# A kernel whose instruction order is planned at build time, planned with other durations

## Chip, cores and metric

One core of one Trainium2 chip runs the whole kernel in one launch. The metric is the device time of an execution in microseconds (us); less is better. The kernel before was timed three times.

## What is computed

A batch of one, 256 tokens by 1024 channels, in float32, goes through two blocks. The first has four layers, each a residual around a mixer: a convolution mixer (layer A), forgetting attention (B), a short convolution (C), and the convolution mixer again (A). The second has two layers, each a token mixer of two attentions and then a feed-forward part with a short convolution.

```
for i in range(4):                      # first block
    kind 0: x = x + conformer_conv_mixer(rms_norm(x, a_norm[j]), ...)       # 31 taps, 2048 channels
    kind 1: x = x + forgetting_attention_mixer(rms_norm(x, b_norm[j]), ...) # 16 heads of 128
    kind 2: x = x + short_conv_mixer(rms_norm(x, c_norm[j]), ...)           # 3 taps
for l in range(2):                      # second block
    x = layer_norm(ALPHA * x + g1 * token_mixer(x * (1 + sc1) + sh1), ...)
    x = layer_norm(ALPHA * x + g2 * conv_ffn(x * (1 + sc2) + sh2), ...)     # 2 x 2816 channels, 3 taps
```

## The kernel before

**Recording and planning.** The Python program does not issue instructions as it goes. Every operation is recorded as an `Op` (`Graph.add`, line 162) with the engine or engines that may run it, a duration that `cost` (line 514) or `mm` (line 624) gives it, the operations it needs, and a key. The key is `Graph.clock`, the sum of the durations of the products recorded so far, plus a shift in microseconds. `Graph.schedule` (line 208) then plays the whole program through: whenever an engine is free, `pick` (line 285) gives it the ready operation with the lowest key whose buffers can be had. An operation is ready when what it needs has ended in the plan and a latency has passed: `SELF`, `CROSS` and `TO_PE` (lines 125 to 127) hold these by engine; for a DMA it is 1.9 us to ACT, DVE or Pool and 2.1 us to TensorE. `issue` (line 457) writes the instructions out in the planned order of start. On the chip each engine runs its own list in that order and waits on semaphores. So a duration in the plan never reaches the chip as a time: it decides the order on each engine, the engine of the few operations that have a choice, the buffer slots, and how many idle products are put in.

**What the plan leaves open.** When TensorE has nothing ready, `schedule` may add an idle product (`idle_op`, line 432), a small product of zeros that nobody reads. An operation with two engines goes to the second if the first would be later (`pick`).

**The work.** Weights come by DMA from SP in tiles of 128x1024 float32 (`need`, line 647), into five slots `wr`. A weight tile is then split into a high and a low part: ACT copies it to `wh` (rounded), and the difference goes to `wl`. The difference is DVE's work, or that of DVE or Pool in layers A and C (`FLEX`, line 577). A product of 128x128 by 128x256 is made of three: high by high, high by low, low by high (`mm3`, line 635). In layer A, 13 of 24 pairs of chunks skip the split and use plain float32 products (`NATIVE_A`, line 550), so that each of the two layers A has 38 tiles whose difference may be on either engine. The DMA of a tile has a key three `LEAD` (4.45 us, line 552) ahead of its product, and the split one.

**Layer A's convolution** (`conv`, line 1023). The last taps of a channel chunk are products on ACT (tile `tap`) that Pool adds up (tile `C`); DVE then adds the first taps on top, in PSUM (tile `po`) and back into `C`. The first of these DVE instructions reads two SBUF tiles, the others one. All these have keys `CONV` (33.45 us, line 553) late. TensorE then sums `C` over the channels (`sums`).

**Layer C** also works out a position bias for later (`bias_block`, line 995): DVE writes masks (`msk`, SBUF to SBUF), TensorE multiplies them with a table.

**Modulation** (`modulate_all`, line 930): 192 DMAs of 128x512 (tile `wa`, two slots) each feed one DVE instruction, beside layer B and the first token mixer.

```
    def need(src, kind="split"):
        with G.late(-3 * LEAD):
            w = G.tile("weights", [128, 1024], F32, "wr", "wr")
            sp.dma_start(w, src)
...
        with G.late(-LEAD):
            a.activation(h, w, AF.Copy)
            (dp if flex[0] else v).tensor_tensor(l, w, h.bitcast(F32), op=OP.subtract)
        return [h, l]
```

Of the kernel before, what the change touches and what calls it, by code (L numbers as in the profile page):

```python
# [9 lines left out]
F32R = mybir.dt.float32r  # L10
# [11 lines left out]
class Buf:  # L22
    """A tile before it has a place: what its instructions are is known, not yet when they run."""
# [8 lines left out]
class View:  # L32
    """A part of a tile: the same steps lead to it in numpy's indices and, later, in the tile's."""
# [58 lines left out]
    def region(self):  # L92
        """First and last partition, and first and last element in them."""
        a = self.arr
        off = a.__array_interface__["data"][0] - self.buf.start
        row = self.buf.row
        p, f = divmod(off, row)
        ext = sum((n - 1) * s for n, s in zip(a.shape[1:], a.strides[1:]))
        return p, p + a.shape[0], f, f + ext + 1
# [16 lines left out]
class Op:  # L116
    __slots__ = ("i", "choices", "key", "need", "outs", "bufs", "fresh", "table", "group", "start", "end", "eng", "waits", "args", "kw",
                 "fn", "done", "margin", "base", "hurry", "act")


class Graph:
    """Instructions with what they need of each other, put in an order that keeps the engines busy."""

    # from the end of an instruction to the start of one that needs it
    SELF = {"PE": 0.0, "DVE": 0.127, "ACT": 0.153, "Pool": 0.102, "DMA": 0.0}
    CROSS = {"PE": 0.2, "DVE": 0.15, "ACT": 0.15, "Pool": 0.12, "DMA": 1.9}
    TO_PE = {"DVE": 0.3, "ACT": 0.36, "Pool": 0.25, "DMA": 2.1}
    # TensorE's clock doubles after a window with so much work for the array, and halves after one with so little
# [33 lines left out]
    def add(self, choices, fn, outs, ins, args, kw, key=None, group=None):  # L162
# [8 lines left out]
        o.table = TABLE.get(args[2]) if fn == "activation" else None  # L171
        o.bufs = []
        pe = choices[0][0] == "PE"

        def meets(e, r, psum):
            # a bank counts as one, save for TensorE alone
            return psum and not (pe and e[4]) or e[0] < r[1] and r[0] < e[1] and e[2] < r[3] and r[2] < e[3]
# [30 lines left out]
    def schedule(self):  # L208
# [14 lines left out]
        # an accumulating product may begin with any of its parts: each may claim the bank  # L223
# [30 lines left out]
        def turn(t):  # L254
            """Goes on to the window of time t."""
            nonlocal tick, load, warm, after
            n = int(t / self.TICK)
            while tick < n:
                warm = load >= self.DOWN if warm else load >= self.UP
                tick, load, after = tick + 1, after, 0.0  # L260

        def room(o):
            """Whether the tiles that begin with this instruction can have their slots."""
            for b in o.bufs:
                if b.slot is not None or b.tag not in free:
                    continue
                n = len(free[b.tag])
                q = queue[b.tag]
                while q and q[0][2].slot is not None:
                    heapq.heappop(q)  # L270
                if n == 0 or (n <= self.reserve.get(b.tag, 1) and q[0][2] is not b):
                    return b.tag
            return None
# [3 lines left out]
        def blocked(o, e, t):  # L277
            """Whether something more urgent comes up before this would be through."""
            end = t + dict(o.choices)[e]
            for w, k, i in soon[e]:  # L280
                if t < w < end - self.HOLD[1] and w < t + self.HOLD[0] and not ops[i].done and k < o.key[0] - self.HOLD[2] and room(ops[i]) is None:
                    return True
            return False
# [57 lines left out]
        latest, count = 0.0, len(ops)  # L341
        t = 0.0
# [3 lines left out]
        while left or events:  # L346
            for e in ENG:
# [25 lines left out]
                if e == "PE":  # L373
                    turn(t)
                    work = o.act
                    if not warm:
                        d = max(0.107, 2 * d)
                        work *= 2
                    over = min(work, max(0.0, t + work - (tick + 1) * self.TICK))
                    load += work - over  # L380
                    after += over
                o.start, o.end = t, t + d
# [49 lines left out]
    def idle_op(self, tag):  # L432
        """A product of zeros that nothing reads: it keeps TensorE's clock up while there is nothing to do."""
# [6 lines left out]
        o.need, o.group, o.outs, o.done, o.table, o.margin, o.hurry = set(), None, [ps], False, None, 0.0, 0.0  # L440
# [49 lines left out]
class Engine:  # L490
    """Records an engine's instructions; their first argument, or out, is what they write."""
# [21 lines left out]

def cost(eng, fn, out, ins, args, kw):
    """The time of an instruction, about, in microseconds."""
    if eng == "DMA":
        some = out if isinstance(out, View) else ins[0]
        return max(0.45, some.shape[0] * some.numel() * 4 / 350e3)
# [61 lines left out]
def program(G, A, V):  # L580
# [43 lines left out]
    def mm(out, w, m, group=None):  # L624
        n = m.numel()
        if m.dtype == F32:
            us = max(0.214, 0.005 + n / 600.0)
        else:
            us = max(0.107 if n < 128 or m.dtype == BF else 0.056, 0.0025 + n / 2400.0)
# [41 lines left out]
    def dense(ps, half, src, kind="split", m=None):  # L671
        """One chunk of 128 outputs, channels by tokens, into half a bank."""
# [15 lines left out]
    def tokens512(srcs, m=None):  # L688
        """512 outputs, tokens by channels: a bank for each half of the tokens."""
# [15 lines left out]
    class Out:  # L705
        """1024 outputs of a product over n chunks, in four banks; the last chunks bank by bank."""
# [27 lines left out]
        def finish_chunks(self, on_chunk):  # L734
            """Chunk by chunk; what is left of the last one goes to a bank of its own, to be added to the rest."""
# [83 lines left out]
    def sums(st, i, src, grp, n):  # L819
        """Adds a chunk's sums over channels, over n, to the columns 2i, 2i+1 of st, a row for each token."""  # L820
# [4 lines left out]
    def rows(cols, n):  # L825
        """[128 tokens, n] columns, as a row for each pair of them, the same on every partition."""
# [6 lines left out]
    class Sums:  # L833
        """Means over channels, of chunks of which all but the last two are added up first."""
# [23 lines left out]
    def raw_tiles(kind):  # L858
        """Places for the next layer's input before its division by the norm, which its first products take."""
# [29 lines left out]
    def mean_rstd(st, eps):  # L889
        """From columns of means and of means of squares, the mean and 1/std of each token as rows."""  # L890
# [8 lines left out]
    def residual(out, gain=None, i0=0, late=0.0, raw="split"):  # L899
        """Adds a mixer's output to x, and takes the next layer's norm."""  # L900
# [29 lines left out]
    def modulate_all(l, after, step, late):  # L930
        """A modulation's columns, a sum over a row of weights each."""
# [20 lines left out]
    def positions():  # L952
# [9 lines left out]
        # the steps of the bias from bucket to bucket, 8 times as large, in three bfloat16 parts  # L962
# [32 lines left out]
    def bias_block(t, i0, n):  # L995
        """The bias (8 times as large) of the queries of half t and the keys 4 i0 .. 4 (i0 + n)."""
# [13 lines left out]
    def layer_a(j, raw):  # L1010
# [12 lines left out]
        def conv(c):  # L1023
            """The last taps by products on ACT and sums on Pool, then the rest on top by DVE, in PSUM."""
# [85 lines left out]
    def softmax(lt, t, p, scale, bias_of=None):  # L1110
        """Exponentials of a head's logits for 128 queries, over their sum."""
# [19 lines left out]
    def head(logits, vt, scale, p, alloc, bias_of=None):  # L1131
        """One head: logits(out, t, n) writes those of 128 queries."""
# [16 lines left out]
    def layer_b(raw):  # L1149
# [14 lines left out]
        def forget():  # L1164
# [18 lines left out]
            # rows of -c and c for every head, in three bfloat16 parts on partitions 0, 32 and 64  # L1183
# [143 lines left out]
    def residual_norm(out, l, gi, gain, shift, nxt):  # L1327
        """x = norm(x + g y), and the next product's input from it; x is kept ALPHA times as large."""
# [39 lines left out]
    def mixer(l):  # L1368
# [20 lines left out]
        # indexer queries, and the chunk of indexer keys and rope keys  # L1389
# [19 lines left out]
        # latent queries and keys  # L1409
# [24 lines left out]
        # queries of the selected attention  # L1434
# [4 lines left out]
        # scores of the keys, and the 64 best of them  # L1439
# [67 lines left out]
        # keys and values of the selected attention, and the gates, beside the attention itself  # L1507
# [170 lines left out]
def layouts(i):  # L1678
    """The inputs as the kernel reads them: transposed, permuted and repeated, never changed."""
# [132 lines left out]
```

## Time and profile before

| | us |
|---|---|
| three timed runs | 1862.46, 1865.36, 1860.3 |
| their median | 1862.46 |
| the profiled execution, span from its first to its last instruction | 1860.9 |

The page gives no other time for the profiled execution than its span; what lies around the span is not shown, and 1860.9 lies among the three runs. Every recorded instruction is issued from one helper, so that all have line L487, and tiles tell them apart: `pd`, `pa` and `po` are PSUM banks, `wr`, `wh`, `wl` a weight tile and its parts, `hh`, `hl`, `ph`, `pl` the parts of the other factor, `C`, `tap`, `U` the convolution's, `idle` the idle products. In time the stages are layer A from 0 to about 200 us, B to 545, C to 815, A to 1000, then mixer, feed-forward, mixer (from 1465), feed-forward (from 1660).

### The profile page before, as it was taken

The page shows a single profiled execution, that of the slowest core. Times are in us where ns is not written, and L with a number is a line of the kernel's source. Part 1 is how long each engine was busy: PE and PEld are TensorE (multiplying, and loading weights), DVE is VectorE, ACT ScalarE, POOL GpSimd, SP SyncE. Part 2 cuts the span into 40 slices and gives each one's busy share as a digit, 9 for nine tenths or more (in the row PEclk, how much of TensorE's full clock was granted, in tenths as well). Part 3 has the DMA queues.
Part 4 walks back from the last instruction along what each step waited for, and adds up shares of the span by engine and source line. Part 5 has one row for each costly group of instructions (what it writes and reads, how often), then busy time and mean ns, then how long its engine had stood idle before and what let it go on. Part 6 is the DMA issues. An engine that isn't in the chain of part 4 may idle for free.

```text
span 1860.9 us, 37322 instructions
## 1 busy us (share of the span) xinstructions
PE 1792.5 (96%) x14150; PEld 1718.2 (92%) x14150; DVE 1498.7 (81%) x3251; ACT 1117.2 (60%) x1985; POOL 418.8 (23%) x487
## 2 busy tenths in 40 slices
PE   9989999999999999999889999999999999999998
PEld 8878999988898989999889988999999989999998
DVE  7998989877768766679999788799887885687766
ACT  6876555544554433468766657946555568766554
POOL 4998401000011032039984100000000100000000
PEclk9999999999999999999999999999999999999999
DMA  7433557877734544543336657666876343446661
GB/s 246 136 114 136 190 188 235 254 250 257 237 117 150 181 159 159 190 150 104 123 125 202 205 176 228 218 228 207 260 253 200 137 139 123 137 136 214 189 191 54
DMA packets 107172, 334.91 MB, mean 180 GB/s; under 512 B 12784, under 2 KB 13168, under 8 KB 106992
## 3 DMA queue, kind: packets, MB, share of 16 engines
q1 hardware_dynamic: 106992, 332.52, 55.2%
q8 instruction: 111, 1.82, 0.4%
q14 instruction: 69, 0.57, 0.1%
HBM read 331.43 MB, written 1.05 MB: 179 GB/s over the span
## 4 chain that ended last, share of the span: by engine, by line
PE 54%; DVE 8%; POOL 3%; ACT 3%; DMA 3%; issue 2%; ACTq 0%; POOLq 0%; SPq 0%; DVEq 0%
PE pd L487 33%; PE po L487 17%; PE pa L487 4%; POOL C L487 3%; DMA wa<-in_w_ada 2%; DVE po L487 2%; DVE wl L487 2%; PE idle L487 1%; ACT wh L487 1%; DVE wa L487 1%; ACT tap L487 1%; DVE msk L487 1%; DVE x L487 1%; DVE IQ L487 0%; ACT L487 0%
## 5 line engine op out<-in xcount | busy, mean ns | idle before, releaser
L487 ACT ACTIVATE wh<-wr 128x1024 fp32r<-128x1024 f32 x478 | 502.7, 1057 | 435.8 <-PE pd L487 289.9
L487 PE MATMUL pd<-hh,wh 128*128 128x256 f32 x2456 | 694.9, 285 | 4.8 <-DVE up L487 1.5
L487 PE MATMUL pd<-hh,wl 128*128 128x256 f32 x2456 | 686.0, 283 | 13.2 <-DVE wl L487 13.2
L487 DVE TENSOR_TENSOR wl<-wr,wh 128x1024 fp32r<-128x1024 f32 x452 | 567.6, 1262 | 155.5 <-ACT wh L487 153.4
L487 PE MATMUL pd<-hl,wh 128*128 128x256 f32 x2456 | 686.0, 282 | 1.5 <-DVE hl L487 1.5
L487 PEld LDWEIGHTS pd<-hh,wl 128*128 128x128 f32 x2456 | 465.6, 191 | 14.3 <-DVE wl L487 13.6
L487 PEld LDWEIGHTS pd<-hh,wh 128*128 128x128 f32 x2456 | 466.3, 190 | 10.1 <-ACT up L487 2.5
L487 PEld LDWEIGHTS pd<-hl,wh 128*128 128x128 f32 x2456 | 464.7, 190 | 4.4 <-DVE hl L487 1.9
L487 POOL TENSOR_TENSOR C<-C,tap 128x233 f32<-128x233 f32 (+16 forms) x364 | 263.2, 748 | 57.8 <-ACT tap L487 48.3
L487 PE MATMUL po<-pl,wh 128*128 128x256 f32 x904 | 253.8, 284 | 2.5 <-DVE pl L487 2.5
L487 PE MATMUL po<-ph,wh 128*128 128x256 f32 x904 | 255.8, 284 | 0.3 <-DVE ph L487 0.3
L487 PE MATMUL po<-ph,wl 128*128 128x256 f32 x904 | 255.4, 283 | 0.0
L487 DVE SCALAR_TENSOR_TENSOR po<-U,vec,po 128x246 f32<-128x246 f32 (+20 forms) x532 | 214.9, 469 | 1.1
L487 ACT ACTIVATE tap<-U,vec 128x227 f32<-128x227 f32 (+17 forms) x364 | 159.7, 480 | 49.2 <-POOL C L487 29.8
L487 PE MATMUL pd<-hn,wr 128*128 128x256 f32 x768 | 179.2, 388 | 1.0 <-DVE U L487 1.0
L487 PEld LDWEIGHTS po<-pl,wh 128*128 128x128 f32 x904 | 170.6, 190 | 2.8 <-DVE pl L487 2.8
L487 PEld LDWEIGHTS po<-ph,wh 128*128 128x128 f32 x904 | 171.5, 190 | 0.8 <-PE idle L487 0.6
L487 PEld LDWEIGHTS po<-ph,wl 128*128 128x128 f32 x904 | 171.7, 190 | 0.0
L487 PEld LDWEIGHTS pd<-hn,wr 128*128 128x128 f32 x768 | 145.1, 193 | 19.7 <-DVE U L487 1.1
L487 POOL TENSOR_TENSOR r<-r,neghalf 128x4 f32<-128x4 f32 (+1 forms) x22 | 28.2, 1281 | 315.7 <-DVE r L487 217.7
L487 POOL TENSOR_TENSOR wl<-wr,wh 128x1024 fp32r<-128x1024 f32 x26 | 63.0, 2424 | 152.0 <-ACT wh L487 150.0
L487 DVE CUSTOM_DVE_ANT_0 wa<-wa,scr,mods 128x512 f32<-128x512 f32 x96 | 72.3, 753 | 27.4 <-DMA wa<-in_w_ada 26.2
(273 smaller groups left out, 2540.2 us busy)
## 6 DMA issues: line engine op xcount, KB each, us to landing
wr<-in_a_in SPq DMA_DIRECT2D x96, 512.0 KB, 3.6
wa<-in_w_ada SPq DMA_DIRECT2D x192, 256.0 KB, 3.7
wr<-in_w_up SPq DMA_DIRECT2D x88, 512.0 KB, 4.4
wr<-in_c_in SPq DMA_DIRECT2D x64, 512.0 KB, 3.6
wr<-in_m_in SPq DMA_DIRECT2D x64, 512.0 KB, 4.0
wr<-in_b_in SPq DMA_DIRECT2D x48, 512.0 KB, 4.4
wr<-in_w_dn SPq DMA_DIRECT2D x44, 512.0 KB, 4.4
wr<-in_a_out SPq DMA_DIRECT2D x32, 512.0 KB, 4.2
```

The lines of the kernel that those rows point to most:

```text
L487: getattr(eng[o.eng], o.fn)(*args, **kw)
```

## The change

The durations that the planner uses are replaced, and a resource is added. A DMA's data is taken to be there 2.75 us (2.85 for TensorE) after its transfer instead of 1.9 (2.1), and a transfer runs at 340 GB/s instead of 350, with a least time of 0.2 us instead of 0.45. A split product over 256 columns takes 0.450 ns a column if its moving tile is a constant buffer and 0.462 ns otherwise (over 512 columns as well), instead of 0.0025 us and 2400 columns a us. A bfloat16 product of 128 columns or more has a lower least time. And Pool's `tensor_tensor` and those DVE instructions that read two SBUF tensors, or copy or scale from SBUF to SBUF, share a port in the plan: an instruction that is given to its engine while the other holds the port is made longer by the rest of the other's time. `pick` does not look at the port. Comments and docstrings are dropped. The rest of the program, its constants among it, is the same.

```diff
-    CROSS = {"PE": 0.2, "DVE": 0.15, "ACT": 0.15, "Pool": 0.12, "DMA": 1.9}
-    TO_PE = {"DVE": 0.3, "ACT": 0.36, "Pool": 0.25, "DMA": 2.1}
+    CROSS = {"PE": 0.2, "DVE": 0.15, "ACT": 0.15, "Pool": 0.12, "DMA": 2.75}
+    TO_PE = {"DVE": 0.3, "ACT": 0.36, "Pool": 0.25, "DMA": 2.85}
...
         o.table = TABLE.get(args[2]) if fn == "activation" else None
+        o.port = shared_port(choices[0][0], fn, outs, ins)
...
+        port = 0.0
         t = 0.0
         self.order = []
...
+                if e == "Pool" or e == "DVE" and o.port:
+                    if o.port and port > t:
+                        d += port - t
+                    if o.port:
+                        port = t + d
                 o.start, o.end = t, t + d
...
+def shared_port(eng, fn, outs, ins):
+
+    if eng == "Pool" or not outs:
+        return fn == "tensor_tensor"
+    sb = [x.numel() > 1 and x.buf.pool != "psum" for x in ins]
+    return eng == "DVE" and (sum(sb) > 1 or fn in ("tensor_scalar", "tensor_copy") and all(sb) and outs[0].buf.pool != "psum")
...
-        return max(0.45, some.shape[0] * some.numel() * 4 / 350e3)
+        return max(0.2, some.shape[0] * some.numel() * 4 / 340e3)
...
-            us = max(0.107 if n < 128 or m.dtype == BF else 0.056, 0.0025 + n / 2400.0)
+            us = max(0.107 if n < 128 else 0.039 if m.dtype == BF else 0.056, 0.0025 + n / 2400.0)
+            if m.dtype == F32R and n >= 256:
+                us = n * (0.450e-3 if m.buf.pool == "const" else 0.462e-3)
```

## Rows read from the trace of the kernel before

**Rows 1.** The page's first part: the span, and each engine's busy time.
```profile
span 1860.9 us, 37322 instructions
PE 1792.5 (96%) x14150; PEld 1718.2 (92%) x14150; DVE 1498.7 (81%) x3251; ACT 1117.2 (60%) x1985; POOL 418.8 (23%) x487
```

**Rows 2.** The chain that ended last, in feed-forward one: start, us, what.
```profile
1298.55 5.47 PE pd L487 x48
1304.03 2.81 PE po L487 x24
```

**Rows 3.** TensorE's waits, whole kernel: us in total, times, longest.
```profile
PE pd L487 <- DVE wl L487: 13.2, 3, 6.1
PE pa L487 <- DVE hd L487: 7.4, 8, 1.7
PE pa L487 <- DVE C L487: 7.3, 7, 2.9
PE pa L487 <- DVE msk L487: 6.1, 4, 1.5
PE pa L487 <- POOL r L487: 4.2, 6, 1.5
PE pa L487 <- DVE p L487: 2.9, 5, 1.1
PE po L487 <- DVE pl L487: 2.5, 1, 2.5
```

**Rows 4.** Timeline, first layer A: start, us, engine, what; DVE, then Pool, then TensorE.
```profile
135.28 6.88 DVE L487 TENSOR_TENSOR wl<-wr,wh 128x1024 fp32r<-128x1024 f32 x1
...
135.56 2.34 POOL L487 TENSOR_TENSOR wl<-wr,wh 128x1024 fp32r<-128x1024 f32 x1
137.87 3.21 POOL L487 TENSOR_TENSOR C<-C,tap 128x230 f32<-128x230 f32 x5
...
142.21 0.80 PE L487 MATMUL pd<-hh,wl 128*128 128x256 f32 x2 [6.10 <-DVE wl L487]
```

**Rows 5.** The same, second layer A: DVE, then TensorE.
```profile
932.20 8.71 DVE L487 TENSOR_TENSOR wl<-wr,wh 128x1024 fp32r<-128x1024 f32 x1
...
940.96 1.01 PE L487 MATMUL pd<-hh,wl 128*128 128x256 f32 x3 [5.91 <-DVE wl L487]
```

**Rows 6.** All of tile wr's and of tile msk's DVE instructions: ns minimum/median/maximum.
```profile
L487 DVE TENSOR_TENSOR wl<-wr,wh x452: 1207/1224/8710, 20.1 to 1830.6; 128x1024 fp32r<-128x1024 f32 x151
...
L487 DVE TENSOR_SCALAR msk<-posf,post x96: 268/280/2364, 325.4 to 748.9; 128x128 bf16<-128x128 f32 x96
```

**Rows 7.** Windows by time: us, busy (count) of PE, PEld, DVE, ACT, POOL; clock.
```profile
139.00:146.00 7.00, 3.79 (x17) 3.79 (x18) 7.00 (x12) 1.61 (x3) 3.05 (x6) 0.52 0.38 131
```

**Rows 8.** Timeline: masks in layer C, `pl` in the second layer A.
```profile
659.68 2.82 DVE L487 TENSOR_SCALAR msk<-posf,post 128x128 bf16<-128x128 f32 x3 [0.34 <-PE pa L487]
...
659.99 2.42 POOL L487 TENSOR_TENSOR wl<-wr,wh 128x1024 fp32r<-128x1024 f32 x1 [0.23 <-DVE msk L487]
...
992.64 2.57 DVE L487 TENSOR_TENSOR pl<-n,ph 128x256 fp32r<-128x256 f32 x1
...
992.53 2.40 POOL L487 TENSOR_TENSOR wl<-wr,wh 128x1024 fp32r<-128x1024 f32 x1 [0.89 <-PE pd L487]
```

**Rows 9.** Pool's groups: first layer A (0 to 200), second (815 to 1000).
```profile
L487 POOL TENSOR_TENSOR wl<-wr,wh 128x1024 fp32r<-128x1024 f32 x7 | 16.6, 2368 | 1.1 <-ACT wh L487 1.1
...
L487 POOL TENSOR_TENSOR wl<-wr,wh 128x1024 fp32r<-128x1024 f32 x6 | 14.9, 2491 | 1.4 <-PE pd L487 0.9 <-ACT wh L487 0.6
```

**Rows 10.** DMA issues (count, KB each, median us from issue to landing).
```profile
wr<-in_a_in SPq DMA_DIRECT2D x96, 512.0 KB, 3.6
...
wr<-in_w_up SPq DMA_DIRECT2D x88, 512.0 KB, 4.4
```

**Rows 11.** Tile wa: DVE's waits for it (us, times), and its DMAs' landing.
```profile
  DMA wa<-in_w_ada: 53.5, 63
...
DMA to landing us min/median/max: 2.3/3.7/7.4
```

More of the change, by code (lines that the diff above doesn't have):

```diff
@@ L117 @@
     __slots__ = ("i", "choices", "key", "need", "outs", "bufs", "fresh", "table", "group", "start", "end", "eng", "waits", "args", "kw",
-                 "fn", "done", "margin", "base", "hurry", "act")
+                 "fn", "done", "margin", "base", "hurry", "act", "port")
 class Graph:
     SELF = {"PE": 0.0, "DVE": 0.127, "ACT": 0.153, "Pool": 0.102, "DMA": 0.0}
-    CROSS = {"PE": 0.2, "DVE": 0.15, "ACT": 0.15, "Pool": 0.12, "DMA": 1.9}
-    TO_PE = {"DVE": 0.3, "ACT": 0.36, "Pool": 0.25, "DMA": 2.1}
+    CROSS = {"PE": 0.2, "DVE": 0.15, "ACT": 0.15, "Pool": 0.12, "DMA": 2.75}
+    TO_PE = {"DVE": 0.3, "ACT": 0.36, "Pool": 0.25, "DMA": 2.85}
     TICK, UP, DOWN = 4.096 / 1.2, 2.56, 1.28
@@ L439, in idle_op @@
         o.base = o.key = (0.0, o.i)
-        o.need, o.group, o.outs, o.done, o.table, o.margin, o.hurry = set(), None, [ps], False, None, 0.0, 0.0
+        o.need, o.group, o.outs, o.done, o.table, o.margin, o.hurry, o.port = set(), None, [ps], False, None, 0.0, 0.0, None
         o.bufs, o.fresh = [ps.buf, w.buf], []
```

## The prediction

> **What bounds the kernel now.** I read the page's busy shares first. TensorE is busy 96% of the span, DVE 81%, ACT 60%, Pool 23% [rows 1]: the kernel is made of products, and only what makes TensorE wait can be won by another order. Second, the chain that ended last shows what a product costs when nothing disturbs it. In the feed-forward parts it is nothing but products, 48 in 5.47 us and 24 in 2.81 us [rows 2], so 0.1140 and 0.1171 us each. There is nothing to win there. Third, TensorE's waits: the list is short, 43.6 us in its seven longest entries, and nearly all are waits for DVE [rows 3]. Fourth, the timeline around the largest two. In the first layer A a DVE subtraction `wl`, which has a median of 1.224 us [rows 6], lasted from 135.28 to 142.16, and TensorE stood still 6.10 us for it. All that time Pool added SBUF tiles without a pause: its own `wl`, then five taps, to 141.08; DVE ended 1.08 us later [rows 4]. The second layer A repeats it, 8.71 us and a wait of 5.91 us [rows 5]. Behind such a wait the granted clock falls: 0.52 of full from 139 to 146 [rows 7], nearly all of it at the level of 1.2 GHz; from 142.2 to 146 products ran at half pace, some 2 us lost, so 4 us for both. The same collision in small stands in layer C: a mask, 0.28 us at the median and 2.36 at worst [rows 6], is held behind a Pool `wl` (three masks in 2.82 us while Pool subtracted) [rows 8], four times in TensorE's list [rows 3].
>
> **The change, part by part.** No duration of the plan reaches the chip. The work stays the same but for idle products and for the engine of single `wl` and sums; what can change is order.
>
> *Longer products.* For 256 columns the plan took 0.0025 + 256/2400 = 0.1092 us; now 0.1152 (constant buffers) and 0.1183. The chip has 0.1140 and 0.1171 [rows 2], so the plan was 4 and 7% short and is now 1% long. On the chip this removes nothing. The keys grow with it, while `LEAD` stays 4.45 us: 38.6 products ahead instead of 40.8, a quarter of a microsecond less, for the split and threefold for the DMA. Only one of the three waits for `wl` is not a collision, at 13.2 - 6.10 - 5.91 = 1.2 us [rows 3, 4, 5]; this slack covers the loss. Where the order gets truer, the waits for `hd` and `r`, mostly in layer B, could shrink (7.4 + 4.2 = 11.6 us [rows 3]); a shuffled order could as well double them. Ends -11.6 and +11.6. I take 0, as these are chains between engines whose own durations are not changed.
>
> *Later landings.* A weight tile was planned at 524288 B / 350 GB/s + 1.9 = 3.40 us, now 1.54 + 2.75 = 4.29; the trace has 3.6 to 4.4 [rows 10]. For `wa` it was 2.65, now 3.52, beside a median of 3.7 [rows 11]. DVE stood 53.5 us, 63 times, in front of `wa` [rows 11], and what is queued behind it on DVE waits too. An honest landing puts other DVE work ahead. But TensorE felt little: its waits there are mainly those for `p`, 2.9 us [rows 3]. Ends 0 and -2.9; I take -1.5. SP's queue keeps its order within a pool of slots and is bound by free slots; I cost its reordering at nothing, since TensorE's seven longest waits name no DMA [rows 3]; without that cover one late tile costs the 0.9 us by which landings were misjudged.
>
> *Port, one Pool instruction ahead.* Where a DVE instruction meets a single Pool subtraction, the new charge is right: 2.82 us for three masks, and 2.57 for `pl` behind the `wl` that began 0.11 us before it [rows 8]. The plan now knows that these come late and gives TensorE other products first. That is the four waits for `msk`, 6.1 us, and the one for `pl`, 2.5 [rows 3]: -8.6, between 0 (the products offered instead are late as well) and -8.6. I take all, because in layer C TensorE has `po` products at hand.
>
> *Port, a train.* At 135.28 the charge would have been only the tap then running, 135.56 - 135.28 = 0.28 us, where DVE really lost 5.7 [rows 4]. The planner lets the two alternate; the chip let Pool go on. So the 6.10 + 5.91 + 4 = 16 us of the two large events are won only as far as the plan's ready times move. Ends 0 and -16. I take the part that one instruction explains, 2.34 of 6.88 us [rows 4], a third: -5.4. Likewise for the waits on `C`, 7.3 us [rows 3], a third, -2.5, ends 0 and -7.3.
>
> The Trainium skill, page "SBUF — State Buffer", section "SBUF: two separate sides", says that Pool and a DVE instruction with two SBUF inputs share a port pair as an exclusive lock, held for one whole instruction by whichever started first. The trace agrees that one blocks the other and not that it ends with one instruction: DVE waited through six [rows 4]. By that rule the train would be charged in full, and the sum would hold the third rival's figure.
>
> *Given back.* A new order of some thousands of instructions makes new waits. Nearest row: a collision in layer A, about 6 us [rows 4, 5]. I take one slightly smaller, +3.5, with ends 0 and +12 (two).
>
> **Sum:** -1.5 - 8.6 - 5.4 - 2.5 + 3.5 = -14.5 us. The profiled execution's span is 1860.9 us, which makes 1846.4; the median of the runs shown lies 1.6 above that span, so 1848.
>
> **Rivals.**
>
> *Only the places move.* The planner charges the port but does not avoid it, so that new collisions replace the old. For: `pick` is blind to the port, and Pool's `wl` come from the same rule. Against: the four masks are charged exactly. Time: 1862.
>
> *Slower: Pool gets more subtractions in layers A.* DVE's longer planned instructions make `pick` find DVE late more often, and the tile goes to Pool. There a `wl` takes 2.37 to 2.49 us against 1.22 [rows 6, 9], holds the port as long and leaves taps behind that run as a train. Layers A had 7 + 6 = 13 [rows 9] of 76 possible. These 13 cost TensorE 6.10 + 5.91 + 2.5 + 4 = 18.5 us [rows 3, 4, 5, 7], 1.4 each. With twenty more: +28 - 14.5 = +13.5, so 1876. It decides from ten more (14.5/1.4), and is visible from fourteen. Against: Pool also becomes busier in the plan, which keeps it from taking tiles.
>
> *All of the port is won.* If every collision is planned as it happens, the port terms go in full: 8.6 + 16 + 7.3 = 31.9, and with the landings 1.5, 1862.5 - 33.4 = 1829. It is what the rule of the Trainium skill's page "SBUF — State Buffer" would bring. Against it stand the six Pool instructions of [rows 4].
>
> That the change does not do what it says is a small case: an order that came out the same would give 1862, inside the first rival.
>
> **How the numbers follow.** Forecast 0.50, places only move 0.18, slower 0.20, all of the port 0.12. The forecast's own range, with the train between 0 and -16 and new waits between 0 and 12, is 1838 to 1857. The range over the cases reaches from below the third rival, 1824 (the `C` and `wa` waits in full and some of layer B's), to the slower one's 1876. A difference of 0.3%, 5.6 us, is about what a measurement of this kernel can tell from none; the three runs spread over 5. Faster: 0.12 + nearly all of 0.50, 0.60; same: 0.18 and a little, 0.19; slower 0.21.
>
> **What would show it.** Right: no TensorE wait for `msk` and `pl`; DVE's waits for `wa` under 20 us; the feed-forward chain still 5.47 and 2.81; Pool's `wl` in layers A near 13, with the longest DVE `wl` well under 8.7 us. Wrong: more than 23 `wl` of Pool there, or DVE instructions over 5 us beside Pool trains with TensorE waiting; or new waits of layer B's kind beyond 11.6 us, which would say that the truer product lengths cost slack that the old, short ones had left.

## The result, and the profile after

The kernel after takes 1831.83 us (median of 4 runs, 1829.68 to 1840.08) beside 1863.51 us for the kernel before (4 runs): the ratio is 0.9837, 95% interval 0.9812 to 0.9861, so 1.6% faster. The forecast was 1848: right in sign, with less than half of the gain. The time lies in the range over all cases, 1824 to 1876, but below the forecast's own range of 1838 to 1857, and, as the experiments show, it came largely for other reasons than mine.

The first part of the page of the kernel after:

```profile
span 1829.3 us, 38072 instructions
PE 1799.9 (98%) x14515; PEld 1725.9 (94%) x14515; DVE 1487.1 (81%) x3260; ACT 1117.5 (61%) x1986; POOL 417.6 (23%) x478
```

Beside [rows 1] the span is 31.6 us shorter. TensorE's 365 further instructions are idle products (851 instead of 486), and nine instructions went from Pool to DVE; the rest of the work is the same. The feed-forward chain (start, us, what) is what it was in [rows 2]:

```profile
1262.15 2.81 PE po L494 x24
1264.96 5.47 PE pd L494 x48
```

TensorE's waits in the kernel after (us in total, times, longest), to be read beside [rows 3]:

```profile
PE pa L494 <- DVE C L494: 3.4, 3, 2.1
PE idle L494 <- ACT Z L494: 2.4, 2, 2.2
PE pa L494 <- POOL r L494: 2.2, 2, 1.9
PE pa L494 <- DVE sel L494: 1.9, 2, 1.3
PE idle L494 <- DVE x L494: 1.8, 1, 1.8
PE pd L494 <- POOL wl L494: 1.4, 2, 1.1
PE pd L494 <- DMA wr<-in_a_in: 1.4, 1, 1.4
```

The seven longest add to 14.5 us instead of 43.6. The waits for `wl` on DVE, `hd`, `msk` and `pl` are gone. The instructions behind them, in the views of [rows 6] and [rows 11]: DVE's subtractions and masks (ns minimum/median/maximum), DVE's waits for `wa` (us, times).

```profile
L494 DVE TENSOR_TENSOR wl<-wr,wh x458: 1204/1225/3389, 20.7 to 1799.3; 128x1024 fp32r<-128x1024 f32 x153
...
L494 DVE TENSOR_SCALAR msk<-posf,post x96: 268/281/584, 302.6 to 726.9; 128x128 bf16<-128x128 f32 x96
...
  DMA wa<-in_w_ada: 27.2, 34
```

No subtraction is held for 7 or 9 us any more, no mask for 2.4, and the 53.5 us in front of `wa` are halved. The mean granted clock rose from 0.984 to 0.991 of full.

**Where the time went.** For the table I took in each trace the start of the last product that the program records for a layer; a stage is the time from one to the next. A is the whole convolution layer, the output part included; M and F are mixer and feed-forward part. All in us, from each run's profiled execution. By this measure the first layer A ends at 252 us in the kernel before and the second at 1042, later than in the rough stages given with its profile. The first stage begins 14.3 to 17.9 us after the start of the span, and the last ends 8 to 9 us before its end; these parts are not in the table.

| run | A1 | B | C | A2 | M1 | F1 | M2 | F2 |
|---|---|---|---|---|---|---|---|---|
| before | 237.9 | 310.4 | 248.0 | 231.5 | 216.3 | 192.2 | 207.5 | 194.6 |
| after | 235.2 | 300.0 | 239.3 | 224.2 | 211.8 | 192.7 | 211.1 | 191.9 |
| port_only | 236.4 | 308.8 | 249.1 | 227.9 | 211.3 | 193.1 | 206.6 | 191.0 |
| products_only | 236.6 | 321.2 | 239.3 | 229.1 | 222.7 | 195.0 | 212.0 | 191.6 |
| landings_only | 228.7 | 298.9 | 250.5 | 225.4 | 211.4 | 195.0 | 205.7 | 193.9 |
| without_port | 230.9 | 301.1 | 239.4 | 227.2 | 213.6 | 193.2 | 211.6 | 191.8 |
| without_products | 234.7 | 306.1 | 248.3 | 229.5 | 210.1 | 194.7 | 210.7 | 191.7 |
| without_landings | 234.9 | 324.7 | 239.8 | 240.0 | 215.9 | 192.1 | 211.6 | 192.1 |
| landing_wa | 235.6 | 293.0 | 250.4 | 232.8 | 210.4 | 194.5 | 208.9 | 192.5 |
| landing_weights | 233.7 | 308.6 | 249.6 | 227.8 | 213.8 | 191.7 | 207.7 | 193.1 |
| landings_no_pool_c | 229.7 | 298.3 | 240.8 | 225.4 | 209.7 | 193.3 | 209.4 | 191.6 |
| after_no_pool_wl | 227.6 | 303.5 | 237.5 | 217.8 | 210.7 | 194.5 | 210.4 | 191.5 |
| no_port_no_pool_wl | 228.8 | 301.7 | 239.0 | 226.4 | 212.7 | 193.2 | 210.2 | 192.1 |
| after_no_idle | 237.9 | 300.5 | 238.4 | 228.0 | 210.3 | 192.1 | 211.4 | 192.5 |

The change took 10.4 us from B, 8.7 from C, 7.3 from A2 and 4.5 from M1. From the first layer A, which had one of the two large collisions, it took 2.7; M2 became 3.6 us longer. The stages also show how much an order scatters where nothing is at stake: F1 and F2 lie between 191 and 195 in every run.

### The profile page after: what moved, and what is told of

Read it like the earlier page. It is cut to its first block, busy times and chain, and to the rows that moved or that the text cites. A ratio compares the mean times of both kernels' runs of the same rounds, so it can differ in the third digit from the quotient of the medians.

```text
span 1829.3 us, 38072 instructions
## 1 busy us (share of the span) xinstructions
PE 1799.9 (98%) x14515; PEld 1725.9 (94%) x14515; DVE 1487.1 (81%) x3260; ACT 1117.5 (61%) x1986; POOL 417.6 (23%) x478
## 4 chain that ended last, share of the span: by engine, by line
PE 79%; DVE 10%; ACT 4%; DMA 2%; POOL 2%; issue 2%; SPq 0%; POOLq 0%; DVEq 0%; ACTq 0%
PE pd L494 49%; PE po L494 22%; PE pa L494 7%; DVE po L494 4%; DVE wl L494 2%; PE idle L494 1%; POOL C L494 1%; ACT wh L494 1%; ACT L494 1%; DMA wa<-in_w_ada 1%; DVE IQ L494 1%; DMA wr<-in_a_in 1%; ACT tap L494 1%; DVE m L494 0%; DMA pi<-in_pos 0%
## 5 line engine op out<-in xcount | busy, mean ns | idle before, releaser
L494 ACT ACTIVATE wh<-wr 128x1024 fp32r<-128x1024 f32 x478 | 502.8, 1058 | 387.0 <-PE pd L494 239.0
L494 PE MATMUL pd<-hh,wl 128*128 128x256 f32 x2456 | 678.2, 281 | 1.4 <-POOL wl L494 1.4
L494 PE MATMUL pd<-hl,wh 128*128 128x256 f32 x2456 | 677.9, 280 | 0.3 <-DVE hl L494 0.3
L494 PEld LDWEIGHTS pd<-hh,wl 128*128 128x128 f32 x2456 | 459.5, 189 | 3.0 <-POOL wl L494 1.8
L494 POOL TENSOR_TENSOR C<-C,tap 128x233 f32<-128x233 f32 (+15 forms) x364 | 276.0, 784 | 42.2 <-ACT tap L494 32.3
L494 DVE SCALAR_TENSOR_TENSOR po<-U,vec,po 128x251 f32<-128x251 f32 (+19 forms) x532 | 217.6, 472 | 2.2
L494 PE MATMUL pd<-hn,wr 128*128 128x256 f32 x768 | 175.2, 382 | 1.3 <-DVE U L494 1.3
L494 POOL TENSOR_TENSOR acc<-acc,x 128x256 f32<-128x256 f32 x12 | 9.3, 777 | 336.6 <-DVE x L494 336.0
L494 POOL TENSOR_TENSOR wl<-wr,wh 128x1024 fp32r<-128x1024 f32 x20 | 50.3, 2513 | 154.4 <-ACT wh L494 154.3
```

Source lines behind the costliest of these rows:

```text
L494: getattr(eng[o.eng], o.fn)(*args, **kw)
```

## Experiments

### One part alone, one part left out

Six kernels: each of the three parts alone, and each left out. The edits against the kernel after, in the order port, products, landings (the parts alone take two of them):

```diff
-                if e == "Pool" or e == "DVE" and o.port:
+                if False:
...
-            us = max(0.107 if n < 128 else 0.039 if m.dtype == BF else 0.056, 0.0025 + n / 2400.0)
-            if m.dtype == F32R and n >= 256:
-                us = n * (0.450e-3 if m.buf.pool == "const" else 0.462e-3)
+            us = max(0.107 if n < 128 or m.dtype == BF else 0.056, 0.0025 + n / 2400.0)
...
-"DMA": 2.75} ... "DMA": 2.85}
-        return max(0.2, some.shape[0] * some.numel() * 4 / 340e3)
+"DMA": 1.9} ... "DMA": 2.1}
+        return max(0.45, some.shape[0] * some.numel() * 4 / 350e3)
```

**port_only.** 

> The shared port alone is added to the plan; products and landings keep the old durations. Theory P (the charge for the port carries the gain): 20 us or more of the 31.7 us, so 1843 us or less, with no TensorE wait for masks and no DVE subtraction over 4 us. Theory L (the truer product lengths carry it): 1855 us or more, with layer B as long as before (310 us) and the second layer A's projection near 175 us. Theory B (only a plan that is right in both brings it): 1850 to 1865 us.

Measured: 1852.78 us, ratio 0.9934 (0.9916 to 0.9952). That is in theory B's range and less than theory P asked, and the four waits for masks are all there, in TensorE's waits of this run:

```profile
PE pa L494 <- DVE msk L494: 6.1, 4, 1.6
PE pa L494 <- POOL r L494: 5.9, 3, 2.0
```

**products_only.** 

> The longer products alone. Theory P: within 5 us of 1863.5, the two long DVE subtractions of layers A still there. Theory L: 1843 us or less, with layer B shorter by 8 us or more and the waits for hd and r gone, masks still waited for (6 us). Theory B: 1850 to 1862 us.

Measured: 1875.04 us, ratio 1.0057 (1.0043 to 1.007): slower than the kernel before, which no theory had. Layer C fell to 239.3 us, but B, M1 and M2 grew by 10.8, 6.4 and 4.5. And the collision in the first layer A became worse: TensorE's waits, and the DVE subtraction behind the longest.

```profile
PE pd L494 <- DVE wl L494: 10.1, 1, 10.1
PE pa L494 <- POOL r L494: 9.6, 7, 4.7
PE pa L494 <- DVE hd L494: 6.9, 12, 1.3
...
133.39 10.74 DVE L494 TENSOR_TENSOR wl<-wr,wh 128x1024 fp32r<-128x1024 f32 x1
```

**landings_only.** 

> The later landings alone. All theories: 1858 to 1866 us, as TensorE hardly waits for DMAs; DVE's waits for the modulation's weights fall from 53.5 us to about 30. If it is below 1855, the landings are a term of their own that I put at 1.5 us.

Measured: 1834.24 us, ratio 0.984 (0.9823 to 0.9857). The part that I had put at 1.5 us brings as much as the whole change. DVE's waits for `wa` fell to

```profile
  DMA wa<-in_w_ada: 7.9, 9
```

and layer B to 298.9 us. The masks still collide (C at 250.5 us). The time is below the 1855 us that were named as the sign of a term of its own.

**without_port.** 

> The change without the port: longer products and later landings. Theory P: it loses most of the gain, 1850 us or more. Theory L: it keeps most, 1840 us or less. Theory B: 1848 to 1860 us.

Measured: 1840.18 us, ratio 0.9869 (0.985 to 0.9889), at theory L's bound. Its interval overlaps that of the whole change: what the port adds to the other two is not told apart from nothing.

**without_products.** 

> Port and later landings, with the old short products. If the parts add (port -12, landings -30, products +11 us alone), 1822 to 1830 us and the best so far, with layer C slow (249 us) since the products alone shortened it. If the port's and the landings' gains are the same waits, 1832 to 1845 us.

Measured: 1847.15 us, ratio 0.99 (0.9879 to 0.9921). The parts don't add: alone, port and landings gave 0.7 and 1.6%, together 1.0%. It is slower than either branch had: added to the landings alone (interval 0.9823 to 0.9857), the port costs some 0.6%. C is slow again (248.3 us), as expected.

**without_landings.** 

> Port and longer products, with the old early landings. If the landings carry the gain: 1855 to 1870 us, with layer B at 308 us or more and DVE's waits for the modulation's weights over 40 us. If the port and the products together can do it: 1845 us or less.

Measured: 1874.72 us, ratio 1.0047 (1.0026 to 1.0068). Without the landings the other two make the kernel slower, beyond the range named; layer B takes 324.7 us, and DVE waits 56.1 us in front of `wa`. The landings carry the gain.

### Which landing

On the kernel before, 0.85 us (0.75 for TensorE) are added to the latency of one kind of DMA; for the second kernel `"wr"` stands for `"wa"`. The transfer times stay as they were; that part of the landings was not tried by itself.

```diff
                     s = (self.SELF if e2 == e else self.TO_PE if e2 == "PE" else self.CROSS)[e]
+                    if e == "DMA" and o.outs and o.outs[0].buf.tag == "wa":
+                        s += 0.85 if e2 != "PE" else 0.75
```

**landing_wa.** 

> The kernel before, with later landings in the plan for the modulation's weights (tile wa) alone. If DVE's waits in front of wa are what the landings saved: layer B near 300 us instead of 310 and the first mixer near 211, so 1845 to 1850 us in all, the layers A unchanged. If the order merely fell better: no such place, 1855 to 1868 us.

Measured: 1844.78 us, ratio 0.9878 (0.9859 to 0.9898). Layer B went from 310.4 to 293.0 us and M1 from 216.3 to 210.4, where the `wa` are; layers A by less than 2.5 each. This is the place that was named beforehand; the total lies 0.2 us below the range named.

**landing_weights.** 

> The kernel before, with later landings for the weight tiles wr alone. If the landings saved by wa: layer B stays at 308 to 312 us, and the total is 1850 to 1866 us, whatever layers A do. If the wr landings are the cause: 1845 us or less with B near 300.

Measured: 1849.55 us, ratio 0.9916 (0.9895 to 0.9937). B stayed at 308.6 us, and the total lies at the lower end of the range named with that. But the gain is clear of noise. It lies in small pieces, A1 -4.2, A2 -3.7, M1 -2.5, B -1.8, and I have no single wait that explains it. The two kinds alone add to 2.1%, more than both together bring (1.6%).

How a wait for `wa` reaches TensorE stands in the timeline of the kernel before, in layer B: DVE, Pool, TensorE (start, us, what, idle before it and its releaser).

```profile
349.57 0.75 DVE L487 CUSTOM_DVE_ANT_0 wa<-wa,scr,vec 128x512 f32<-128x512 f32 x1 [1.65 <-DMA wa<-in_w_ada]
350.25 0.08 DVE L487 DVE_READ_ACCUMULATOR2_ANT mods<- 128x1 f32 x1
350.25 0.22 DVE L487 TENSOR_SCALAR r<-pa 128x2 f32<-128x2 f32 x2
...
350.64 1.35 POOL L487 TENSOR_TENSOR r<-r,neghalf 128x4 f32<-128x4 f32 x1 [35.49 <-DVE r L487]
...
352.05 0.65 PE L487 MATMUL pa<-cst,r 128*128 128x128 f32 x4 [1.53 <-POOL r L487]
```

DVE stood 1.65 us in front of a modulation row that nobody needed yet. Behind it in DVE's list was the norm of a head (`r`), then Pool's power, then TensorE's product, which waited 1.53 us. In the list of waits this is "POOL r", not a DMA. With the `wa` planned later, DVE's waits for them in layer B (before, then landing_wa) fell, and TensorE's waits in layer B are a single entry:

```profile
DVE wa L487 <- DMA wa<-in_w_ada: 33.1, 42, 2.2
...
DVE wa L489 <- DMA wa<-in_w_ada: 8.0, 9, 1.6
...
PE pa L489 <- POOL r L489: 3.5, 7, 1.4
```

The 7.4 us for `hd` are gone with nothing but the landing of `wa` changed. In the kernel before, all eight waits for `hd` and four of those for `r` in layer B end less than 6 us after DVE had stood in front of a `wa`; in landing_wa none does. TensorE's waits are not the whole gain there: they fell by 8 us (7.4 + 4.2 to 3.5) and the layer by 17.4. In the kernel before the granted clock was also 0.51 from 262 to 269 us, ahead of the first use of a `wa` (271.5), by estimate 3.4 us, where landing_wa has 1.00 over the whole layer; the other 6 us I have not traced.

### Pool's subtractions in layer C

The kernel before with the later landings, and

```diff
-FLEX = "aoc"
+FLEX = "ao"
```

**landings_no_pool_c.** 

> The kernel before with the later landings, and no subtraction on Pool in layer C. If the masks behind Pool's subtractions are what layer C loses: C takes 239 to 242 us instead of 250.5, TensorE waits for no mask, and the total is 1822 to 1829 us, below both kernels. If the longer products shortened C in another way: C stays at 247 us or more and the total at 1830 to 1838.

Measured: 1824.5 us, ratio 0.9792 (0.9764 to 0.9821), with C at 240.8 us instead of 250.5, and no mask among TensorE's waits. So C loses by the collision. The truer products had shortened it by another distribution, in products_only 8 subtractions on Pool in C instead of 13, at other moments: with them C takes 237.5 to 239.8 us in every run, and without them 248.0 to 250.5 in every run that has subtractions on Pool there. The port, which I had expected to do it, did not.

### Pool's subtractions in the convolution's chain

Why did the collisions' end bring so little in layers A? Pool's timeline at the end of the first convolution, kernel after:

```profile
176.97 2.38 POOL L494 TENSOR_TENSOR wl<-wr,wh 128x1024 fp32r<-128x1024 f32 x1
179.28 0.70 POOL L494 TENSOR_TENSOR C<-C,tap 128x232 f32<-128x232 f32 x1
179.92 2.43 POOL L494 TENSOR_TENSOR wl<-wr,wh 128x1024 fp32r<-128x1024 f32 x1
182.28 8.90 POOL L494 TENSOR_TENSOR C<-C,tap 128x231 f32<-128x231 f32 x6
```

DVE in the same time, to the end of the last channel chunk:

```profile
182.20 1.23 DVE L494 TENSOR_TENSOR wl<-wr,wh 128x1024 fp32r<-128x1024 f32 x1 [5.36 <-ACT wh L494]
...
184.07 3.37 DVE L494 TENSOR_TENSOR wl<-wr,wh 128x1024 fp32r<-128x1024 f32 x2 [0.18 <-ACT wh L494]
187.72 2.94 DVE L494 TENSOR_TENSOR wl<-wr,wh 128x1024 fp32r<-128x1024 f32 x2 [0.28 <-ACT wh L494]
...
193.18 0.15 DVE L494 COPY C<-po 128x3 f32<-128x3 f32 x1
```

The same last copy in the kernel before:

```profile
192.12 0.15 DVE L487 COPY C<-po 128x3 f32<-128x3 f32 x1
```

Two subtractions stand in front of Pool's last taps, and DVE's subtractions then stretch six taps to 8.90 us. The last piece of `C` comes at 193.18 us; in the kernel before it came at 192.12. The projections end 10.7 us sooner (185.5 instead of 196.2), and TensorE then runs idle products until `C` is there. The end of the layer is then bound by Pool's and DVE's chain, not by TensorE's wait. That goes with the port: in the five runs that have it beside subtractions on Pool, the last `C` of the first layer A comes 6 to 10 us after the last projection starts; in the eight runs without it, the kernel before among them, it comes 3 to 15 us before. A kernel tests whether Pool's subtractions do it: the kernel after with `FLEX = ""`, all differences on DVE.

**after_no_pool_wl.** 

> The kernel after, with no subtraction on Pool at all. If Pool's subtractions stand in the convolution's chain at the end of layers A: the last C of the first layer A comes 5 us or more earlier than at 193 us, and the total is 1815 to 1828 us. If DVE is the bound there and misses the help: C's end at 195 us or later, and the total 1832 to 1850.

Measured: 1819.48 us, ratio 0.9766 (0.9739 to 0.9793), below the change's interval: the lowest time of all, though its interval overlaps that of landings_no_pool_c. Pool's taps run without a break,

```profile
159.75 10.85 POOL L494 TENSOR_TENSOR C<-C,tap 128x239 f32<-128x239 f32 x14
```

and DVE has the last `C` some 19 us earlier (two copies, the second the last):

```profile
173.98 0.23 DVE L494 COPY C<-po 128x13 f32<-128x13 f32 x2
```

The layers A fell to 227.6 and 217.8 us. DVE took the 20 subtractions over and did not become the bound: the projections end after the last `C` again (184.4 us).

**no_port_no_pool_wl** (the same, with the port left out as above). 

> The kernel after without the port and with no subtraction on Pool: longer products and later landings alone, beside the 1819.5 us with the port. If the charge for the port helps once Pool's subtractions no longer stand in the convolution's chain: 1825 to 1835 us. If the port does nothing then: 1815 to 1823. If it still costs through idle products and DVE's order: below 1815.

Measured: 1829.62 us, ratio 0.9814 (0.9792 to 0.9837), as the first branch had it. With Pool free of subtractions the charge for the port is worth about 0.5%, nearly all in A2 (217.8 against 226.4 us); the intervals just touch. Without the port, taking Pool's subtractions away shortens the two layers A by 2.9 us together (from 230.9 and 227.2); with it, by 14.0. So it is beside the port that they cost most there.

### Idle products

```diff
-WARM = True
+WARM = False
```

**after_no_idle.** 

> The kernel after without idle products. If they only fill waits and keep the clock: 1850 us or more, with a lower mean clock. If the planner's charge for the port makes it put in products that delay real ones: the output part of the first layer A is shorter by 5 us or more than 64.3, and the total within 10 us of 1832.

Measured: 1837.52 us, ratio 0.9857 (0.9831 to 0.9883), mean clock 0.973 instead of 0.991. Neither: the output part of the first layer A takes 66.7 us instead of 64.3, so there is no sign that the idle products delay anything there, and without them only some 0.2% are lost, which is not told apart from none.

## Why the prediction was right, and where it was not

The sign was right, and of the mechanism one part: what changes is the order on DVE, and TensorE's waits go. The size and the place were not. The measured 1831.83 us lies below the forecast's own range, 1838 to 1857, whose ends move one term at a time; all of its ends at once would give 1834 to 1862, which does not hold it either.

**Longer products.** I took 0, between -11.6 and +11.6. Alone they measured +0.57%, and inside this lie two large terms of opposite sign: -8.7 us in C, which I had booked under the port, and +21.7 us in B, M1 and M2. With the later landings beside them B is at 301.1 us (without_port), so the loss in B belongs to the pair of longer products and too early landings. Why products planned longer make DVE stand before `wa` at worse places I have not traced. The sign that the prediction named for this, new waits of layer B's kind beyond 11.6 us, is there in products_only (9.6 + 6.9 us for `r` and `hd`) and in without_landings (18.5 for `r`). In M2 every run that has them takes 210.2 to 212.0 us, those without 205.7 to 210.7, so a few us may be theirs. That there is nothing to win in the feed-forward parts held: F1 and F2 differ by 0.5 and 2.7 us between the two kernels.

**Later landings: the term that failed.** I took -1.5 with an end of -2.9, since "TensorE felt little: its waits there are mainly those for `p`". Alone they measured -1.6%, some 30 us. The modulation's rows alone, in landing_wa, brought 22.8 us (0.0122 of 1865.5) and the weight tiles alone, in landing_weights, 15.7; the two do not add, and only of the first do the runs show by what wait it came, and that in part. The step was wrong in one inference: I looked for DVE's 53.5 us of waits [rows 11] under the name of DMA or of the stage's own products. DVE runs its list in order, and behind `wa` stood the head's norm and other work of the layer, so that TensorE's waits bore the names `hd` and `r`. Those 11.6 us I had seen in [rows 3], and priced at 0 under another part. And I costed the reordering of the weight tiles at nothing because no DMA stood in that list, by the same inference.

**Port, one instruction ahead.** I took -8.6, of it 6.1 for masks, because the charge is right there and TensorE has other products at hand. In the kernel after the waits are gone; but of the six kernels with one part alone or one left out, the masks' waits are all there in the three without the longer products, and gone in the three with them. The one for `pl` is gone in the three with the port and stays in the three without it (1.4 to 2.4 us): of the 8.6 us, these 2.5 are the port's. `pick` does not look at the port, and an exact charge for a mask that is already chosen does not keep Pool from its subtraction; that reason is read from the program, and no run tests it.

**Port, a train.** I took a third, -5.4, and -2.5 for `C`. The long subtractions did go (at most 3.4 us instead of 8.7), with the port alone (3.36) but with the landings alone too (2.77). And their price was misread: the projections of the first layer A shortened by 10.7 us, and its output part grew by 8.3 (56.0 to 64.3), because the last `C` came when it had come before. TensorE's wait in the middle of a layer is no price if another chain ends the layer.

**Given back.** I took +3.5. M2 is 3.6 us longer. The size fits by luck: it was a guess, and M2 is the stage that is long in the runs with the longer products.

**Rivals.** "All of the port is won", 1829, has the measured number and not the cause: the port alone gives 1852.78. What it would rest on is the rule of the Trainium skill (page "SBUF — State Buffer", section "SBUF: two separate sides") that the lock is held for one whole instruction. As a bound on the wait the runs speak against it: a subtraction of 1.2 us was held to 10.74 us in products_only, beyond the 8.71 of [rows 5]. "Slower by more subtractions on Pool" did not come: layers A have 11 instead of 13. Its mechanism was half right: Pool's subtractions do cost, 0.7% of the time (0.9766 without any, 0.9837 with them), but by lengthening Pool's chain. The signs that I named: waits for `msk` and `pl` gone, held; `wa` under 20 us, not (27.2); feed-forward unchanged, held; the longest `wl` well under 8.7, held. "Only the places move", 1862, did not come either, but its reason, that `pick` is blind to the port, fits the masks of port_only. The lower end of the range over all cases, 1824, counts the waits on `C` a second time: the 1829 holds them in full.

Two versions lie below both kernels, for reasons that were named before they ran: the later landings with no subtraction on Pool in C (1824.5 us, its interval overlapping the change's, so not told apart from it), and the change with none on Pool at all (1819.48 us, clear of it).

## What to carry to other kernels

A wait on an engine that works its list in order is paid by whoever needs what stands behind it, under that instruction's name: before a long wait of a side engine is priced at nothing, look up what is queued behind it. A wait of the bounding engine in the middle of a stage is worth its length only if no other chain ends the stage; compare when the last input of the stage's end arrives. And truer numbers in a planner need not help one by one: here one part alone made the kernel slower and another alone brought as much as all three.

## What the runs showed of the hardware

- DVE's subtraction of two SBUF tensors, 1.22 us undisturbed, took 6.88, 8.71 and 10.74 us where Pool's instructions followed one another without a pause. In the case of 8.71 us DVE came in before Pool's train was over, when Pool paused for 0.08 us (939.82 to 939.90); the tap behind the pause took 1.55 us instead of 0.67.
- It goes the other way too. At the end of the first convolution of the kernel after, Pool pauses for 0.08 us behind each of its last taps; six taps took 8.90 us beside five subtractions of DVE, five of them 1.53 to 1.70 us and one 0.69. The first of these subtractions came in at 182.20 us with no pause to be seen, so the pause is not shown to be needed.
- Without idle products the mean clock was 0.973 instead of 0.991, and the time some 0.2% longer, with intervals that overlap. Why so little, I have not traced; the order of the products changed with it.
